# Zero products ahead of the first product, ScalarE's squares behind the weight copies, and the first group by two chunks, in a two-block transformer kernel on one core

## The chip, the cores and the metric

The kernel runs on 1 core of one Trainium2 chip. The metric is the device time of one execution in microseconds (us), the median of several runs. The core's engines are TensorE (PE in the profile; PEld is its weight load), VectorE (DVE), ScalarE (ACT), GpSimd (POOL) and SyncE (SP), which issues nearly all DMAs.

## The reference

A first block (windowed attention and a gated recurrence side by side, then an MLP) and a second block of two layers, on 256 tokens of width 1024 with 16 meta tokens ahead of them. What matters here is the first norm and the first projection:

```python
h = concat([meta_tokens, x])                 # 16 + 256 tokens of 1024
a = h * rsqrt(mean(h * h) + EPS) * norm_mix  # rms_norm
(q_na, k_na, v_na, q_hg, z_f, z_b, i_hg, g_hg, gate_na, gate_hg) = split(a @ w_in)
...                                          # both branches, w_o, MLP, second block
```

## The kernel before, in words

All matrix products run on TensorE from weights that come once from HBM. A weight is read in units of 512 rows by 512 columns (`units`, 1 MB of float32, tile `raw`), and each unit in two halves of two 128-row chunks. ScalarE copies a half into a rounded `whi` (L256), VectorE subtracts the copy from the raw half and leaves `wlo` (L257). The activations are split in the same way into a high part `xh` (ScalarE, L417) and a low part `xl` (VectorE, L418), transposed, so that a product of float32 accuracy is three products: high with high, high with low, low with high. The tokens are two tiles of 128 (t = 0, 1) and the 16 meta tokens; the width 1024 is two groups g of four chunks of 128 (tiles `xh_8`/`xl_9` are g = 0, `xh_10`/`xl_11` g = 1 in the kernel before).

The start runs like this. `norm_in(t)` squares a token tile on ScalarE (L442, a square and a read of its sum), VectorE adds the parts (L433), GpSimd takes the power, VectorE scales (L543, two halves of 512 columns) into `xn`. The scale vector is spread over the partitions by a product of a row of ones with `grow` (L514), which stays in two PSUM banks `g_ps` until the meta tokens are scaled. `split_in(t, g)` transposes four blocks on TensorE (L410) and splits the bank into `xh` and `xl`. `first_split(n)` cuts the nth half of the weights. `meta_in()` does the same for the meta tokens: its eight small transposes on TensorE are L571, and its splits write the last 16 columns of `xh` and `xl`.

The first product group is "gh" (`xstat_unit`, `xstat`: tokens are the stationary operand, 512 columns of weights move): 2 token tiles x 8 chunks x 3 = 48 products into two PSUM tiles. They are evicted by `ev_gh` (ScalarE L582, VectorE L583 and L584). The second group, "kn" (`wstat`, L361 to L363), takes all 272 tokens at once, so its first product needs the meta columns of `xh`, and the first with `xl` the meta columns of `xl`.

The order on each engine is set at build time by a scheduler, from the order in which the code is written, priorities (`urgent`) and `after(...)`, which keeps what is written under it behind given instructions. At run time every engine but TensorE's weight load goes through its own list in that order. The PSUM pool `mp` has four banks, two of them held by `g_ps` at the start. The order of SyncE's DMAs at the start is: first half of h[0], `grow`, second half of h[0], `ident`, first half of the first weight unit (L517), h[1] (L518), second half of that unit (L519), the two halves of the next unit, the meta tokens, `vrow`, the third unit.

Of the kernel before, what the change touches and what calls it, by code (L numbers as in the profile page):

```python
# [9 lines left out]
BF16 = mybir.dt.bfloat16  # L10
# [5 lines left out]
D = 1024  # L16
# [54 lines left out]
def kernel(  # L71
# [26 lines left out]
    def mt(i, shape, dt=F32, name="m"):  # L98
        return slot.tile(shape, dt, name=nm(name), tag=f"m{i}")
# [15 lines left out]
    def mps():  # L115
        return mp.tile([128, 512], F32, name=nm("mp"), tag="mp")
# [114 lines left out]
    for key, tags in BORROW.items():  # L231
        i = [u[0] for u in units].index(key)
# [110 lines left out]
        return [(q[k // 2][0][:, k % 2], q[k // 2][1][:, k % 2]) for k in range(4)]  # L343


    def xstat(ps, xs, ws, first, last):

        n = len(xs)
        for k in range(n):
            (xh, xl), (wh, wl) = xs[k], ws[k]  # L350
            T.matmul(ps, lhsT=xh, rhs=wh, start=first and k == 0, stop=False)  # L351
            T.matmul(ps, lhsT=xh, rhs=wl, start=False, stop=False)  # L352
            last_mm[:] = [T.matmul(ps, lhsT=xl, rhs=wh, start=False, stop=last and k == n - 1)]  # L353

    def wstat(ps, xs, ws, b, first, last):

# [23 lines left out]
    def tok(xT, k, t):  # L380
        hh, ll = xT[k // 4]
        return hh[:, k % 4, 128 * t:128 * t + 128], ll[:, k % 4, 128 * t:128 * t + 128]

    def xstat_unit(keys, xT, evict, budget=None, tfirst=False, ps=None):
        ps = ps or [acc(), acc()]
        if tfirst:
            ws = use(keys[0], budget) + use(keys[1], budget)
            for t in range(2):
                nl = len(later)
                xs = [tok(xT, k, t) for k in range(8)]  # L390
                xstat(ps[t], xs[:TF], ws[:TF], True, False)
                with flushed(nl):
                    xstat(ps[t], xs[TF:], ws[TF:], False, True)
                evict(t, ps[t])
        else:
            for i in range(2):
                ws = use(keys[i], budget)
                nl = len(later)
                for t in range(2):
                    with group():  # L400
                        xstat(ps[t], [tok(xT, 4 * i + k, t) for k in range(4)], ws, i == 0, i == 1)
                    if i == 1:
                        evict(t, ps[t])
                flush(nl)
# [9 lines left out]
    def split_bank(ps, hi, lo, scale=None):  # L414

        if scale is None:
            return (S.activation(out=hi, in_=ps, func=AF.Copy),  # L417
                    V.tensor_tensor(out=lo, in0=ps, in1=f(hi), op=ALU.subtract))  # L418
        else:
            S.activation(out=hi, in_=ps, func=AF.Copy, scale=scale)  # L420
            V.scalar_tensor_tensor(out=lo, in0=ps, scalar=scale, in1=f(hi), op0=ALU.mult, op1=ALU.subtract)
# [15 lines left out]
    def sq_mean(src, accum=None, of=None):  # L437

        n = src.shape[1]
        j = tmp.tile([128, 1024], BF16, name=nm("junk"), tag="junk", bufs=1)  # L440
        a = small([src.shape[0], 1], bufs=8) if accum is None else accum
        S.activation(out=j[0:src.shape[0], 0:n], in_=src, func=AF.Square, scale=float(of or n) ** -0.5, accum_out=a)  # L442
        return a
# [65 lines left out]
    nc.sync.dma_start(out=ident, in_=cst[:, C_ID:C_ID + 128])  # L509
    one_row = cp.tile([1, 128], F32, name="one_row")  # L510
    G.memset(one_row, 1.0)
    g_ps = [mps() for _ in range(2)]
    for k in range(2):
        T.matmul(g_ps[k], lhsT=one_row, rhs=grow[:, 512 * k:512 * k + 512], start=True, stop=True)  # L514
    w0 = rawp.tile([128, 2048], F32, name="raw0", tag="raw")
    w0v = w0.rearrange("p (k n) -> p k n", n=512)
    nc.sync.dma_start(out=w0v[:, 0:2], in_=units[0][1][:, 0:2])  # L517
# [12 lines left out]
          (mt(2, [128, 4, 272], F32R, "xh1"), mt(3, [128, 4, 272], F32R, "xl1"))]  # L530
    xn = [mt(5, [128, D], name="xn0"), mt(6, [128, D], name="xn1"), mt(7, [16, D], name="xnm")]

    def norm_in(t, src, parts):
        p = src.shape[0]
        q = small([p, 3])
        G.memset(q, EPS)
        for i in range(parts):
            n = D // parts
            sq_mean(src[:, n * i:n * i + n], q[:, i:i + 1], D)
        r = rpow(q[:, 0:parts + 1])  # L540
        for i in range(2):
            c = slice(512 * i, 512 * i + 512)
            V.scalar_tensor_tensor(out=xn[t][:, c], in0=src[:, c], scalar=r, in1=g_ps[i][0:p],  # L543
                                   op0=ALU.mult, op1=ALU.mult)

    def split_in(t, g):
        ps = transposes(xn[t][:, 512 * g:512 * g + 512]).rearrange("p (k t) -> p k t", k=4)
        c = slice(128 * t, 128 * t + 128)
        split_bank(ps, xT[g][0][:, :, c], xT[g][1][:, :, c])

    def first_split(n):
        cap[0] = n
# [2 lines left out]

    norm_in(0, h[0], 2)
    first_split(1)
    split_in(0, 0)
    first_split(2)
    norm_in(1, h[1], 1)  # L560
    split_in(1, 0)
    first_split(3)
    split_in(0, 1)
    first_split(4)
    split_in(1, 1)

    def meta_in():
        norm_in(2, hm, 1)
        ps = mps()
        for k in range(8):  # L570
            T.transpose(out=ps[:, 16 * k:16 * k + 16], in_=xn[2][:, 128 * k:128 * k + 128], identity=ident[0:16, 0:16])  # L571
        pv_ = ps[:, 0:128].rearrange("p (k t) -> p k t", k=8)
        for g in range(2):
            split_bank(pv_[:, 4 * g:4 * g + 4], xT[g][0][:, :, 256:272], xT[g][1][:, :, 256:272])
# [1138 lines left out]
```

## Time and profile before

| | |
|---|---|
| median of 3 runs | 845.84 us (845.59 to 846.05) |
| the profiled execution, its own time | 845.33 us |
| its span, first to last instruction | 843.4 us |
| TensorE busy | 828.1 us (98%) |
| VectorE, ScalarE, GpSimd busy | 581.4, 464.4, 59.2 us |
| mean granted TensorE clock in the records | 0.997 |
| first product of "gh" / of "kn" | 11.35 us / 26.91 us |

Times in the views count from the start of the span. "own time" is about 1.9 us longer than the span; what shifts the end of the span shifts it too.

### The profile page before, as it was taken

The page shows a single profiled execution, that of the slowest core. Times are in us where ns is not written, and L with a number is a line of the kernel's source. Part 1 is how long each engine was busy: PE and PEld are TensorE (multiplying, and loading weights), DVE is VectorE, ACT ScalarE, POOL GpSimd, SP SyncE. Part 2 cuts the span into 40 slices and gives each one's busy share as a digit, 9 for nine tenths or more (in the row PEclk, how much of TensorE's full clock was granted, in tenths as well). Part 3 has the DMA queues.
Part 4 walks back from the last instruction along what each step waited for, and adds up shares of the span by engine and source line. Part 5 has one row for each costly group of instructions (what it writes and reads, how often), then busy time and mean ns, then how long its engine had stood idle before and what let it go on. Part 6 is the DMA issues. An engine that isn't in the chain of part 4 may idle for free.

```text
span 843.4 us, 12871 instructions
## 1 busy us (share of the span) xinstructions
PE 828.1 (98%) x5037; PEld 734.7 (87%) x5037; DVE 581.4 (69%) x840; ACT 464.4 (55%) x757; POOL 59.2 (7%) x139
## 2 busy tenths in 40 slices
PE   6999999999999999999999999999999999999996
PEld 4999998888889999999879988888799999888885
DVE  6746667775859976657976868866655557559753
ACT  6456755574556655544775545545566455455442
POOL 2420020001000000000021000000000000020001
PEclk9999999999999999999999999999999999999998
DMA  8863443442549997867727556757155445559521
GB/s 304 259 195 106 151 151 101 160 158 82 199 131 361 373 334 274 299 224 274 258 94 252 198 192 224 257 200 249 67 205 172 154 149 172 165 198 318 175 82 50
DMA packets 88240, 168.02 MB, mean 199 GB/s; under 512 B 4802, under 2 KB 8898, under 8 KB 88180
## 3 DMA queue, kind: packets, MB, share of 16 engines
q1 hardware_dynamic: 87508, 166.66, 58.2%
q8 instruction: 39, 0.64, 0.3%
q10 hardware_dynamic: 288, 0.52, 0.2%
q14 instruction: 21, 0.17, 0.1%
q0 software_dynamic: 384, 0.03, 0.0%
HBM read 166.14 MB, written 1.05 MB: 198 GB/s over the span
## 4 chain that ended last, share of the span: by engine, by line
PE 93%; DVE 2%; DMA 1%; ACT 1%; issue 1%; POOL 0%; SPq 0%; POOLq 0%; DVEq 0%; ACTq 0%
PE acc L351 17%; PE acc L353 17%; PE acc L352 16%; PE acc L362 7%; PE acc L363 7%; PE acc L361 7%; PE mp L363 3%; PE mp L362 3%; PE mp L361 3%; PE mp L410 3%; PE mp L876 1%; DMA h<-in_x_dram 1%; ACT junk L442 1%; PE mp L353 1%; PE mp L351 1%
## 5 line engine op out<-in xcount | busy, mean ns | idle before, releaser
L257 DVE TENSOR_TENSOR wlo<-raw,whi 128x1024 fp32r<-128x1024 f32 x244 | 295.0, 1226 | 140.9 <-ACT whi L256 138.5
L256 ACT ACTIVATE whi<-raw 128x1024 fp32r<-128x1024 f32 x244 | 252.1, 1055 | 166.0 <-PE acc L353 101.3
L477 DVE SCALAR_TENSOR_TENSOR tb<-adw,csil,tb 128x512 f32<-128x512 f32 x96 | 71.1, 747 | 8.9 <-issue 4.9
L362 PE MATMUL acc<-xl,whi 128*128 128x272 f32 (+1 forms) x224 | 64.5, 288 | 0.0
L363 PE MATMUL acc<-xh,wlo 128*128 128x272 f32 (+1 forms) x224 | 64.5, 289 | 0.0
L361 PE MATMUL acc<-xh,whi 128*128 128x272 f32 (+1 forms) x224 | 64.3, 288 | 0.0
L361 PE MATMUL mp<-uh,whi 128*128 128x256 f32 x224 | 63.1, 285 | 0.0
L362 PE MATMUL mp<-ul,whi 128*128 128x256 f32 x224 | 63.0, 283 | 0.0
L363 PE MATMUL mp<-uh,wlo 128*128 128x256 f32 x224 | 62.1, 283 | 0.0
L363 PE MATMUL acc<-oh,wlo 128*128 128x256 f32 x192 | 55.0, 287 | 0.0
L362 PE MATMUL acc<-ol,whi 128*128 128x256 f32 x192 | 54.6, 284 | 0.0
L361 PE MATMUL acc<-oh,whi 128*128 128x256 f32 x192 | 54.4, 283 | 0.0
L351 PE MATMUL acc<-whi,hh 128*128 128x512 f32 x128 | 50.0, 392 | 0.0
L352 PE MATMUL acc<-wlo,hh 128*128 128x512 f32 x128 | 49.9, 390 | 0.0
L353 PE MATMUL acc<-whi,hl 128*128 128x512 f32 x128 | 49.7, 390 | 0.0
L351 PE MATMUL acc<-whi,yT 128*128 128x512 f32 (+1 forms) x128 | 48.5, 379 | 0.0
L352 PE MATMUL acc<-wlo,yT 128*128 128x512 f32 (+1 forms) x128 | 48.3, 377 | 0.0
L353 PE MATMUL acc<-whi,yT 128*128 128x512 f32 (+1 forms) x128 | 48.2, 377 | 0.0
L352 PE MATMUL acc<-wlo,oh 128*128 128x512 f32 x112 | 44.6, 398 | 0.0
L351 PE MATMUL acc<-whi,oh 128*128 128x512 f32 x112 | 44.3, 396 | 0.0
L352 PE MATMUL acc<-wlo,eh 128*128 128x512 f32 x112 | 44.0, 393 | 0.0
L353 PE MATMUL acc<-whi,ol 128*128 128x512 f32 x112 | 43.9, 392 | 0.0
(413 smaller groups left out, 2009.9 us busy)
## 6 DMA issues: line engine op xcount, KB each, us to landing
raw<-in_odd_in_w_dram SPq DMA_DIRECT2D x28, 1024.0 KB, 5.1
adw<-in_ada_w_dram SPq DMA_DIRECT2D x48, 512.0 KB, 6.1
raw<-in_w_in_dram SPq DMA_DIRECT2D x21, 1024.0 KB, 5.2
raw<-in_even_in_w_dram SPq DMA_DIRECT2D x20, 1024.0 KB, 5.1
raw<-in_w_up_dram SPq DMA_DIRECT2D x16, 1024.0 KB, 6.8
raw<-in_w_down_dram SPq DMA_DIRECT2D x16, 1024.0 KB, 7.3
raw<-in_even_out_w_dram SPq DMA_DIRECT2D x8, 1024.0 KB, 5.2
raw<-in_odd_out_w_dram SPq DMA_DIRECT2D x8, 1024.0 KB, 5.5
```

What stands on the lines that cost most here:

```text
L256: S.activation(out=hi.rearrange("p k n -> p (k n)"), in_=r, func=AF.Copy)
L257: V.tensor_tensor(out=lo.rearrange("p k n -> p (k n)"), in0=r, in1=f(hi.rearrange("p k n -> p (k n)")), op=ALU.subtract)
L351: T.matmul(ps, lhsT=xh, rhs=wh, start=first and k == 0, stop=False)
L352: T.matmul(ps, lhsT=xh, rhs=wl, start=False, stop=False)
L353: last_mm[:] = [T.matmul(ps, lhsT=xl, rhs=wh, start=False, stop=last and k == n - 1)]
L361: T.matmul(ps, lhsT=wh[:, c], rhs=xh, start=first and k == 0, stop=False)
L362: T.matmul(ps, lhsT=wh[:, c], rhs=xl, start=False, stop=False)
L363: T.matmul(ps, lhsT=wl[:, c], rhs=xh, start=False, stop=last and k == n - 1)
L410: last_t[:] = [T.transpose(out=ps[:, 128 * b:128 * b + 128], in_=src[:, 128 * b:128 * b + 128], identity=ident)]
L442: S.activation(out=j[0:src.shape[0], 0:n], in_=src, func=AF.Square, scale=float(of or n) ** -0.5, accum_out=a)
L477: V.scalar_tensor_tensor(out=a, in0=w[:, k], scalar=csil[:, kk:kk + 1], in1=a, op0=ALU.mult, op1=ALU.add)
L876: T.matmul(pss[i][:, 128 * hd:128 * hd + 128], lhsT=Kc[:, hd, 128 * i:128 * i + 128], rhs=bass.AP(tensor=q.tensor, offset=q.offset, ap=ap[ ...
```

## The change

Three things are done. (1) A zeroed bfloat16 tile `warm` is multiplied with itself on TensorE, 256 columns at a time, into PSUM banks that nobody reads: 9 products ahead of the two products with `grow`, 4 behind them, 5 behind the first four transposes. (2) ScalarE's squares of h[1] are put behind the first `xh`, those of the meta tokens behind the `xh` of token tile 0, g = 1. (3) For the first token tile and the first unit of "gh", `xstat` goes by two chunks: both high-high products, both high-low, both low-high, then the next two chunks. The number of products of the model is the same.

```diff
-    def xstat(ps, xs, ws, first, last):
+    def xstat(ps, xs, ws, first, last, by=1):
         n = len(xs)
-        for k in range(n):
-            (xh, xl), (wh, wl) = xs[k], ws[k]
-            T.matmul(ps, lhsT=xh, rhs=wh, start=first and k == 0, stop=False)
-            T.matmul(ps, lhsT=xh, rhs=wl, start=False, stop=False)
-            last_mm[:] = [T.matmul(ps, lhsT=xl, rhs=wh, start=False, stop=last and k == n - 1)]
+        for k0 in range(0, n, by):
+            ks = range(k0, k0 + by)
+            for m, (a, b) in enumerate(((0, 0), (0, 1), (1, 0))):
+                for k in ks:
+                    last_mm[:] = [T.matmul(ps, lhsT=xs[k][a], rhs=ws[k][b], start=first and k == 0 and m == 0,
+                                           stop=last and k == n - 1 and m == 2)]
...
-                        xstat(ps[t], [tok(xT, 4 * i + k, t) for k in range(4)], ws, i == 0, i == 1)
+                        xstat(ps[t], [tok(xT, 4 * i + k, t) for k in range(4)], ws, i == 0, i == 1,
+                              2 if keys[0] == ("gh", 0) and not i and not t else 1)
...
+    warm = mt(12, [128, 256], BF16, name="warm")
+    V.memset(warm, 0.0)
+    first = []
+    def warm_up(n):
+        ps = mps()
+        for _ in range(n):
+            with after(first):
+                first[:] = [T.matmul(ps[:, 0:256], lhsT=warm[:, 0:128], rhs=warm, start=True, stop=True)]
+    warm_up(9)
     g_ps = [mps() for _ in range(2)]
     for k in range(2):
-        T.matmul(g_ps[k], lhsT=one_row, rhs=grow[:, 512 * k:512 * k + 512], start=True, stop=True)
+        with after(first):
+            first[:] = [T.matmul(g_ps[k], lhsT=one_row, rhs=grow[:, 512 * k:512 * k + 512], start=True, stop=True)]
+    warm_up(4)
...
-    def norm_in(t, src, parts):
+    def norm_in(t, src, parts, behind=()):
...
-        for i in range(parts):
-            n = D // parts
-            sq_mean(src[:, n * i:n * i + n], q[:, i:i + 1], D)
+        with after(behind):
+            for i in range(parts):
+                n = D // parts
+                sq_mean(src[:, n * i:n * i + n], q[:, i:i + 1], D)
...
-    split_in(0, 0)
+    with after(first):
+        x00 = split_in(0, 0)
+    first[:] = last_t
+    warm_up(5)
     first_split(2)
-    norm_in(1, h[1], 1)
+    norm_in(1, h[1], 1, x00[:1])
     split_in(1, 0)
     first_split(3)
-    split_in(0, 1)
+    x01 = split_in(0, 1)
...
-        norm_in(2, hm, 1)
+        norm_in(2, hm, 1, x01[:1])
```

The built order on SyncE and GpSimd is the same in both kernels. On the other three it differs up to the start of "kn" and a little beyond, and not after that. Numbers behind a name are buffers: in the change `raw_121`, `raw_125`, `raw_131` are the first three weight units, `h_81` and `h_82` the two token tiles, `hm_128` the meta tokens, `mp_157`, `mp_184`, `mp_195`, `mp_206` the transposes of (t, g) = (0, 0), (1, 0), (0, 1), (1, 1), `acc_216` and `acc_217` the sums of "gh". Before, the same are `raw_104`, `raw_108`, `raw_114`, `h_81`, `h_82`, `hm_111`, `mp_140`, `mp_161`, `mp_172`, `mp_183`, `acc_193`, `acc_194`.

ScalarE at the start, from the second square of h[0], in the kernel before:

```order
L442 ACTIVATE junk_128,sm_124<-h_81 128x512
L256 ACTIVATE whi_136<-raw_104 128x1024
L442 ACTIVATE junk_153,sm_151<-h_82 128x1024
L417 ACTIVATE xh_8_117<-mp_140 128x4x128
L256 ACTIVATE whi_147<-raw_104 128x1024
L256 ACTIVATE whi_168<-raw_108 128x1024
L256 ACTIVATE whi_179<-raw_108 128x1024
L442 ACTIVATE junk_269,sm_267<-hm_111 16x1024
L417 ACTIVATE xh_8_117<-mp_161 128x4x128
```

The same place in the change:

```order
L444 ACTIVATE junk_145,sm_141<-h_81 128x512
L256 ACTIVATE whi_153<-raw_121 128x1024
L256 ACTIVATE whi_170<-raw_121 128x1024
L419 ACTIVATE xh_11_134<-mp_157 128x4x128
L444 ACTIVATE junk_176,sm_174<-h_82 128x1024
L256 ACTIVATE whi_191<-raw_125 128x1024
L256 ACTIVATE whi_202<-raw_125 128x1024
L256 ACTIVATE whi_218<-raw_131 128x1024
L419 ACTIVATE xh_11_134<-mp_184 128x4x128
```

The copy of the second half of the first unit now stands ahead of the first `xh`, and the squares of h[1] behind it; the copy of the third unit's first half stands ahead of the second `xh`.

VectorE from the first subtraction to the low part of (t, g) = (1, 0), before:

```order
L257 TENSOR_TENSOR wlo_137<-raw_104,whi_136 128x1024
L433 TENSOR_REDUCE sm_155<-sm_151 128x1
L418 TENSOR_TENSOR xl_9_118<-mp_140,xh_8_117 128x4x128
L543 SCALAR_TENSOR_TENSOR xn_13_122<-h_82,sm_156,mp_100 128x512
L543 SCALAR_TENSOR_TENSOR xn_13_122<-h_82,sm_156,mp_101 128x512
L257 TENSOR_TENSOR wlo_148<-raw_104,whi_147 128x1024
L257 TENSOR_TENSOR wlo_169<-raw_108,whi_168 128x1024
L257 TENSOR_TENSOR wlo_180<-raw_108,whi_179 128x1024
L433 TENSOR_REDUCE sm_271<-sm_267 16x1
L418 TENSOR_TENSOR xl_9_118<-mp_161,xh_8_117 128x4x128
```

The same stretch in the change:

```order
L257 TENSOR_TENSOR wlo_154<-raw_121,whi_153 128x1024
L560 SCALAR_TENSOR_TENSOR xn_15_138<-h_81,sm_148,mp_113 128x512
L257 TENSOR_TENSOR wlo_171<-raw_121,whi_170 128x1024
L420 TENSOR_TENSOR xl_12_135<-mp_157,xh_11_134 128x4x128
L435 TENSOR_REDUCE sm_178<-sm_174 128x1
L257 TENSOR_TENSOR wlo_192<-raw_125,whi_191 128x1024
L560 SCALAR_TENSOR_TENSOR xn_16_139<-h_82,sm_179,mp_112 128x512
L560 SCALAR_TENSOR_TENSOR xn_16_139<-h_82,sm_179,mp_113 128x512
L257 TENSOR_TENSOR wlo_203<-raw_125,whi_202 128x1024
L257 TENSOR_TENSOR wlo_219<-raw_131,whi_218 128x1024
L420 TENSOR_TENSOR xl_12_135<-mp_184,xh_11_134 128x4x128
```

The scaling of h[1] moved behind two more subtractions, and the low part of token tile 1 behind a subtraction of the third unit as well. On TensorE the transposes into `mp_206` wait for that low part, since they take the bank of `mp_184`.

ScalarE at the end of "gh" (`gg` is the eviction, the 128x4x16 rows are the meta columns), before:

```order
L256 ACTIVATE whi_229<-raw_227 128x1024
L256 ACTIVATE whi_233<-raw_227 128x1024
L417 ACTIVATE xh_8_117<-mp_277 128x4x16
L608 ACTIVATE csil<-vc 128x8
L582 ACTIVATE gg_190<-acc_193 128x512
L417 ACTIVATE xh_10_119<-mp_277 128x4x16
L604 ACTIVATE sm_297<-sm_294 128x8
L256 ACTIVATE whi_311<-raw_309 128x1024
L582 ACTIVATE gg_190<-acc_194 128x512
```

The same place in the change:

```order
L256 ACTIVATE whi_252<-raw_250 128x1024
L256 ACTIVATE whi_256<-raw_250 128x1024
L604 ACTIVATE gg_213<-acc_216 128x512
L256 ACTIVATE whi_334<-raw_332 128x1024
L604 ACTIVATE gg_213<-acc_217 128x512
L256 ACTIVATE whi_338<-raw_332 128x1024
L419 ACTIVATE xh_11_134<-mp_300 128x4x16
```

The meta columns moved behind both evictions of "gh" and two copies. On TensorE the eight small transposes that feed them stand ahead of the last 22 of the 48 products before, and behind all 48 in the change. On VectorE the meta columns of `xl` stand behind the subtraction that belongs to `whi_338`.

## Rows read from the trace of the kernel before

**Rows 1.** The page: span, then busy time of each engine.

```profile
span 843.4 us, 12871 instructions
PE 828.1 (98%) x5037; PEld 734.7 (87%) x5037; DVE 581.4 (69%) x840; ACT 464.4 (55%) x757; POOL 59.2 (7%) x139
```

**Rows 2.** Waits of TensorE, whole span: total us, times, longest.

```profile
PE acc L351 <- ACT xh L417: 3.1, 1, 3.1
PE mp L410 <- DVE xn L1228: 1.0, 2, 0.5
```

**Rows 3.** Timeline of ScalarE: start, us, instruction, idle time before it.

```profile
7.68 1.06 ACT L256 ACTIVATE whi<-raw 128x1024 fp32r<-128x1024 f32 x1 [2.23 <-DMA raw<-in_w_in_dram]
9.67 1.06 ACT L442 ACTIVATE junk<-h 128x1024 bf16<-128x1024 f32 x1 [0.94 <-DMA h<-in_x_dram]
10.63 0.19 ACT L442 ACTIVATION_READ_ACCUMULATOR junk<-h 128x1 f32 x1
10.72 0.58 ACT L417 ACTIVATE xh<-mp 128x512 fp32r<-128x512 f32 x1
11.20 1.04 ACT L256 ACTIVATE whi<-raw 128x1024 fp32r<-128x1024 f32 x1
...
21.69 1.05 ACT L256 ACTIVATE whi<-raw 128x1024 fp32r<-128x1024 f32 x1
22.63 0.20 ACT L417 ACTIVATE xh<-mp 128x64 fp32r<-128x64 f32 x1
...
27.11 0.60 ACT L582 ACTIVATE gg<-acc 128x512 f32<-128x512 f32 x1 [0.28 <-PE acc L353]
27.60 1.05 ACT L256 ACTIVATE whi<-raw 128x1024 fp32r<-128x1024 f32 x1
```

**Rows 4.** Timeline of TensorE, 11 to 28 us.

```profile
11.35 0.79 PE L351 MATMUL acc<-whi,xh 128*128 128x512 f32 x1 [3.06 <-ACT xh L417]
...
12.37 0.63 PE L353 MATMUL acc<-whi,xl 128*128 128x512 f32 x1
...
14.08 0.63 PE L351 MATMUL acc<-whi,xh 128*128 128x512 f32 x1
14.50 1.76 PE L410 MATMUL mp<-ident,xn 128*128 128x128 f32 x8
...
17.49 0.40 PE L352 MATMUL acc<-wlo,xh 128*128 128x512 f32 x1
...
18.39 0.39 PE L351 MATMUL acc<-whi,xh 128*128 128x512 f32 x1
...
20.71 0.40 PE L352 MATMUL acc<-wlo,xh 128*128 128x512 f32 x1
...
21.73 0.48 PE L351 MATMUL acc<-whi,xh 128*128 128x512 f32 x1
...
26.68 0.39 PE L353 MATMUL acc<-whi,xl 128*128 128x512 f32 x1
26.91 0.41 PE L361 MATMUL acc<-xh,whi 128*128 128x272 f32 x2
```

**Rows 5.** Timeline of VectorE, 8 to 17 us.

```profile
8.77 1.22 DVE L257 TENSOR_TENSOR wlo<-raw,whi 128x1024 fp32r<-128x1024 f32 x1 [0.97 <-ACT whi L256]
...
11.33 0.69 DVE L418 TENSOR_TENSOR xl<-mp,xh 128x512 fp32r<-128x512 f32 x1 [0.33 <-ACT xh L417]
11.94 1.40 DVE L543 SCALAR_TENSOR_TENSOR xn<-h,sm,mp 128x512 f32<-128x512 f32 x2
13.25 3.49 DVE L257 TENSOR_TENSOR wlo<-raw,whi 128x1024 fp32r<-128x1024 f32 x3
16.66 0.14 DVE L433 TENSOR_REDUCE sm<-sm 16x1 f32<-16x2 f32 x1
```

**Rows 6.** The DMA of L519, the first unit's second half: issue, then its landing.

```profile
3.39 0.44 SPq L519 DMA_DIRECT2D raw<-in_w_in_dram  x1
DMA to landing us min/median/max: 7.5/7.5/7.5
```

More of the change, by code (lines that the diff above doesn't have):

```diff
@@ L548, in split_in @@
         c = slice(128 * t, 128 * t + 128)
-        split_bank(ps, xT[g][0][:, :, c], xT[g][1][:, :, c])
+        return split_bank(ps, xT[g][0][:, :, c], xT[g][1][:, :, c])
     def first_split(n):
```

## The prediction

> **What bounds the kernel now.** I read the page first: TensorE is busy 828.1 of 843.4 us [rows 1]. The reader is to see that there are only some 15 us to win, and that a microsecond lost on TensorE is lost at the end. Then the waits of TensorE over the whole span: one of 3.1 us for the first `xh`, and after that none longer than 0.5 us [rows 2]. Behind the start the kernel therefore runs as fast as TensorE can, and the order there is the same in both kernels, so I take it that a shift of the start of "kn" goes through to the end one for one. The measure of the change is when TensorE gets to "kn": 26.91 us before [rows 4].
>
> The timeline of TensorE [rows 4] shows what the zero products are aimed at. The first products come every 0.43 us (12.37 to 14.08 is four of them), those from 18.39 to 20.71 every 0.232 us (ten). 512 columns in 0.43 us is the lower level of the clock, 1.2 GHz; 0.232 us is close to the upper, 2.4 GHz. Seven products and most of eight transposes (14.50, 1.76 us) ran at the lower level; at the upper they would have taken 7 x 0.232 + 8 x 0.11 = 2.5 us instead of about 4.9 (11.35 to 16.26). So at most 2.4 us is to be won by the clock.
>
> The timelines of ScalarE and VectorE [rows 3, 5] show what feeds TensorE. VectorE works without a pause from 11.33 us on (each row begins where the last ends). TensorE was slow just while its feed was thin, which is why no wait shows there.
>
> **The zero products.** 18 products of 256 columns. By the rows of 512 columns at either level one takes 0.12 to 0.21 us [rows 4]; their weight loads lie beside products there, so I price them at nothing. Nine take 1.0 to 1.9 us ahead of the products with `grow`; should they hold those up by all of it, the first transposes come as much later, and their `xh` has until 11.88 (below) instead of 10.72. The other nine stand in the 3.06 us in which TensorE waits for the first `xh` [rows 4], which grow longer. If the weight loads did not overlap it would be twice that, still inside the gap. The one memset on VectorE comes long before its first subtraction. Cost: 0.
>
> **ScalarE and the first product.** This is where the change costs. ScalarE takes its list in order, and now the copy of the first unit's second half stands ahead of the first `xh`. That half lands at 3.39 + 7.5 = 10.9 us [rows 6], and the order of the DMAs is the same. ScalarE, done with the first copy at 8.74, sits until 10.92. A following instruction starts 0.96 us after a copy or a long square, 0.09 after the read of a sum, 0.48 after an `xh` (starts 9.67, 10.63, 10.72, 11.20) [rows 3]. So: copy 10.92, `xh` 11.88 to 12.46, squares of h[1] 12.36, read 13.32, copy of the second unit's first half 13.41 to 14.47. The first product starts 0.05 us behind `xh`, at 12.5: 1.15 us later than before. The squares of h[1], which started at 9.67, start 2.7 us later.
>
> **VectorE and the second token tile.** Spacing on VectorE: a subtraction 1.137 us ((16.66 - 13.25)/3), a pair of scalings 1.31 (11.94 to 13.25), an `xl` 0.61 (11.33 to 11.94) and 0.69 long [rows 5]. The subtraction for the copy that ends at 14.47 starts at 14.50. Behind it in the new list: scalings of h[1] at 15.64, subtraction at 16.95, another, of the third unit, at 18.08, and only then `xl` of token tile 1, 19.22 to 19.91. The transposes of (1, 1) need the PSUM bank that this `xl` frees, so they start at 19.96. TensorE has by then done 12 products of token tile 0, 8 transposes and 4 more products, which take 12 x 0.232 + 8 x 0.11 + 4 x 0.232 = 4.6 us of the 7.45 us since 12.5. It stands idle about 2.9 us in several pieces: for `xl` of tile 0 (13.2 to 13.9 behind the second subtraction), for `xn` of tile 1 (first half done at about 16.4), for `xh` behind the third unit's copies.
>
> That makes the clock nearly worthless at this place: if the 12 products run at the lower level they take 12 x 0.195 = 2.3 us more, and nearly all of it falls into those waits. By my working 0.2 us comes through.
>
> From 19.96 TensorE runs through: four transposes 0.44 (17.49 to 18.39 less two products), 32 products x 0.232 = 7.43, the small transposes 0.79 (20.71 to 21.73 less one product) [rows 4]. That is 28.6 us, 1.7 us later than 26.91.
>
> **A new wait ahead of "kn".** Before, the meta tokens' small transposes stood 22 products ahead of "kn", and ScalarE split them at 22.63 [rows 3] under cover of those 22 x 0.232 = 5.1 us. Now they stand behind all 48 products, and their split stands on ScalarE behind the second eviction of "gh" and one more weight copy. The last product starts at 27.6 and its result is there 0.39 later (row of 26.68) [rows 4]: 28.0. Eviction 28.0; copy 0.49 behind it (27.11 to 27.60) at 28.5; small `xh` 0.96 behind that, 29.5 to 29.7 [rows 3]. TensorE, ready at 28.6, waits 1.1 us. It then has four products that need `xh` alone, 0.125 us each (26.91, two), up to 30.2. The next needs the meta columns of `xl`, which stand on VectorE behind the subtraction of that same copy: start 29.6 to 29.95 (VectorE comes from an eviction), 1.137 us, then about 0.2 us as for the small `xh`: 30.95 to 31.3. Second wait 0.75 to 1.1 us. TensorE goes on at about 31.15 with four products of "kn" done, as if it had begun at 30.65. Shift: 30.65 - 26.91 = 3.7 us.
>
> **The edit to two chunks** moves two products of `xl` and all use of the second half back, and adds none. What it could save, the wait of the third chunk, lies inside the stretch that VectorE sets. Cost 0. The squares of the meta tokens, now behind the `xh` of tile 0, g = 1, are followed by two more `xh` and subtractions long before the 27.8 at which their transposes come. Cost 0.
>
> **Sum.** 0 + 1.7 + 2.0 = +3.7, with 0 to 0.2 for a low clock: +3.8 us. The profiled execution took 845.33 us by its own time, so 849.1; the median shown is 0.5 above it, and I give the sum on the median: 849.6 us. A difference below 0.2% (1.7 us) counts here as about what a measurement of this kernel cannot tell from none.
>
> **The clock, trace against rule.** The trace shows a wait of 3.06 us ahead of 11.35 and the low level after it [rows 4]. The Trainium skill, "TensorE: Matmul & The Clock Gate", section "Part 1: The HAM clock gate", says that the low level is the default, that sustained activity lifts it, and that idleness brings it back. Here the gap behind the last zero products is longer than before (to 12.5), so by that rule they may buy nothing, and the new waits may even drop the clock later. By the rule the sum is +3.9 to +5.9, without it +3.7.
>
> **Rivals.**
> - *The clock falls again in the new waits.* TensorE idles 2.9 of 7.45 us from 12.5 on, and 2 of 2.5 us ahead of "kn". For it: the kernel before did run a stretch of about 4.6 us at the lower level (11.35 to about 16) [rows 4]. Against: no row shows the clock fall behind it. One more such stretch costs 4.6/2 = 2.3 us where TensorE would have been busy throughout, less where it waits: +5.1 to +5.9, on the median 850.9 to 851.7, about 851.3.
> - *The wait ahead of "kn" is not there* because the scheduler's list is met in another timing (evictions earlier, the copy done under the last products). Against it: the copy stands behind the eviction of the last product. Then only the shift of the start stays: +1.75, 847.6, at the very edge of what can be told.
> - *Not slower: the zero products hold the full clock and TensorE runs without waits from 12.5.* Then "kn" starts at 12.5 + 48 x 0.232 + 12 x 0.11 + 0.79 = 25.75, 1.15 us earlier: 844.7. It decides at the low part of token tile 1, which would have to be there at 17.1 instead of 19.9. Against it: VectorE's list from 8.77 [rows 5] up to that row holds five subtractions, three scalings, an `xl` and a small sum before it, 5 x 1.137 + 3 x 0.655 + 0.61 + 0.07 = 8.3 us, so 17.8 at the end even with no wait at all. To be told from no change it would need 0.5 us more.
>
> **Chances.** Forecast 0.55; clock falls again 0.22; no wait ahead of "kn" 0.12; not slower 0.11. The range takes in the first three, from the lower edge of the third (+1.6) to the upper of the second (+5.8): 847.4 to 851.6. Slower by over 0.2%: 0.55 + 0.22 + 0.07, a little over half of the 0.12, = 0.84. Within 0.2%: the other 0.05 and 0.07 of the last case, 0.12. Faster: 0.04, if that case also finds the 0.5 us.
>
> **What would show it.** In the changed profile: ScalarE idle from 8.7 to 10.9 ahead of its second copy; the first product at about 12.5; `xl` of token tile 1 ending near 19.9 and four transposes right behind it; then on TensorE two waits of about 1 us each at the start of "kn", for ScalarE's `xh` and for VectorE's `xl`; the fifth product of "kn" near 31.15. The clock: spacing of the first products 0.43 or 0.23 us, and no 0.43 behind 20 us. I am wrong if the first unit's second half lands much earlier than 10.9, if "kn" starts without those waits, or if a later part gives the shift back.

## The result, and the profile after

The changed kernel takes 850.1 us (median of 4 runs, 849.71 to 850.36), the kernel before in the same runs 845.72 (845.24 to 846.05). The ratio is 1.0056, 95% interval 1.0044 to 1.0068: 4.4 us slower, more than the 0.2% that this measurement can tell. The profiled execution of the change took 850.36 us. Its page begins:

```profile
span 848.5 us, 12911 instructions
PE 833.4 (98%) x5055; PEld 737.5 (87%) x5055; DVE 580.6 (68%) x841; ACT 464.6 (55%) x757; POOL 55.2 (7%) x139
```

Against [rows 1] the span is 5.1 us longer and TensorE holds 18 products more. The waits of TensorE in the first 40 us (total, times, longest) are now:

```profile
PE acc L353 <- ACT xh L419: 3.6, 3, 2.7
PE mp L523 <- DVE warm L516: 1.2, 1, 1.2
PE acc L362 <- ACT xh L419: 0.9, 1, 0.9
PE acc L363 <- DVE xl L420: 0.7, 1, 0.7
```

In [rows 2] stood one wait for the first `xh`. Now three stand there, and the two at L362 and L363 are the start of "kn". The timeline of ScalarE in the change (start, us, instruction, idle before) shows where the first come from:

```profile
8.41 1.06 ACT L256 ACTIVATE whi<-raw 128x1024 fp32r<-128x1024 f32 x1 [3.06 <-DMA raw<-in_w_in_dram]
10.99 1.06 ACT L256 ACTIVATE whi<-raw 128x1024 fp32r<-128x1024 f32 x1 [1.52 <-DMA raw<-in_w_in_dram]
11.95 0.58 ACT L419 ACTIVATE xh<-mp 128x512 fp32r<-128x512 f32 x1
12.43 1.05 ACT L444 ACTIVATE junk<-h 128x1024 bf16<-128x1024 f32 x1
...
18.59 0.60 ACT L419 ACTIVATE xh<-mp 128x512 fp32r<-128x512 f32 x1 [1.76 <-PE mp L412]
19.08 1.05 ACT L256 ACTIVATE whi<-raw 128x1024 fp32r<-128x1024 f32 x1
20.03 0.59 ACT L419 ACTIVATE xh<-mp 128x512 fp32r<-128x512 f32 x1
...
29.29 0.60 ACT L604 ACTIVATE gg<-acc 128x512 f32<-128x512 f32 x1 [0.28 <-PE acc L353]
29.79 1.05 ACT L256 ACTIVATE whi<-raw 128x1024 fp32r<-128x1024 f32 x1
30.74 0.21 ACT L419 ACTIVATE xh<-mp 128x64 fp32r<-128x64 f32 x1
```

The second copy waits for its half until 10.99, and the first `xh` stands behind it (11.95, in [rows 3] 10.72). At the end one eviction and one copy stand ahead of the meta columns' `xh` at 30.74. TensorE in the same execution:

```profile
12.59 1.22 PE L353 MATMUL acc<-whi,xh 128*128 128x512 f32 x2 [2.69 <-ACT xh L419]
...
17.02 1.05 PE L353 MATMUL acc<-whi,xl 128*128 128x512 f32 x2
17.87 1.12 PE L412 MATMUL mp<-ident,xn 128*128 128x128 f32 x8
19.24 0.50 PE L353 MATMUL acc<-whi,xh 128*128 128x512 f32 x1 [0.25 <-ACT xh L419]
...
21.24 0.60 PE L412 MATMUL mp<-ident,xn 128*128 128x128 f32 x4
...
31.00 0.76 PE L362 MATMUL acc<-xh,whi 128*128 128x272 f32 x4 [0.88 <-ACT xh L419]
32.47 0.39 PE L363 MATMUL acc<-xl,whi 128*128 128x272 f32 x1 [0.70 <-DVE xl L420]
```

All 12 first products came 0.43 us apart (12.59 to 17.87), the lower of the two levels, 1.2 GHz. The transposes of (1, 1) started at 21.24, and VectorE was not what they waited for: its `xl` of token tile 1 ended at 19.96.

```profile
17.01 2.36 DVE L257 TENSOR_TENSOR wlo<-raw,whi 128x1024 fp32r<-128x1024 f32 x2
19.28 0.68 DVE L420 TENSOR_TENSOR xl<-mp,xh 128x512 fp32r<-128x512 f32 x1
...
31.06 1.22 DVE L257 TENSOR_TENSOR wlo<-raw,whi 128x1024 fp32r<-128x1024 f32 x1
32.20 0.22 DVE L420 TENSOR_TENSOR xl<-mp,xh 128x64 fp32r<-128x64 f32 x1
```

"kn" goes on from its fifth product at 32.47, as if it had begun at 32.47 - 4 x 0.125 = 31.97, 5.06 us later than in [rows 4]. That is the whole difference of the spans: nothing is won or lost behind it.

### The profile page after: what moved, and what is told of

Same layout as the page of the kernel before. It is cut to its first block, busy times and chain, and to the rows that moved or that the text cites. A ratio compares the mean times of both kernels' runs of the same rounds, so it can differ in the third digit from the quotient of the medians.

```text
span 848.5 us, 12911 instructions
## 1 busy us (share of the span) xinstructions
PE 833.4 (98%) x5055; PEld 737.5 (87%) x5055; DVE 580.6 (68%) x841; ACT 464.6 (55%) x757; POOL 55.2 (7%) x139
## 4 chain that ended last, share of the span: by engine, by line
PE 92%; DVE 3%; ACT 2%; DMA 1%; issue 1%; POOL 0%; SPq 0%; POOLq 0%; DVEq 0%; ACTq 0%
PE acc L353 49%; PE acc L363 7%; PE acc L364 7%; PE acc L362 7%; PE mp L363 3%; PE mp L362 3%; PE mp L364 3%; PE mp L412 3%; PE mp L353 2%; PE mp L898 1%; DMA raw<-in_w_in_dram 1%; DVE wlo L257 1%; DMA raw<-in_even_in_w_dram 1%; PE mp L734 1%; ACT junk L444 1%
## 5 line engine op out<-in xcount | busy, mean ns | idle before, releaser
L353 PE MATMUL acc<-whi,yT 128*128 128x512 f32 (+1 forms) x256 | 76.6, 378 | 0.0
L363 PE MATMUL acc<-xl,whi 128*128 128x272 f32 (+1 forms) x224 | 64.7, 289 | 0.7 <-DVE xl L420 0.7
L362 PE MATMUL acc<-xh,whi 128*128 128x272 f32 (+1 forms) x224 | 64.2, 289 | 0.9 <-ACT xh L419 0.9
L362 PE MATMUL mp<-uh,whi 128*128 128x256 f32 x224 | 63.1, 285 | 0.0
L363 PE MATMUL mp<-ul,whi 128*128 128x256 f32 x224 | 63.0, 283 | 0.0
L353 PEld LDWEIGHTS acc<-whi,yT 128*128 128x128 f32 x256 | 47.3, 188 | 8.8
L363 PE MATMUL acc<-ol,whi 128*128 128x256 f32 x192 | 54.6, 284 | 0.0
L362 PE MATMUL acc<-oh,whi 128*128 128x256 f32 x192 | 54.4, 283 | 0.0
```

The costliest lines, as they stand in the source:

```text
L353: last_mm[:] = [T.matmul(ps, lhsT=xs[k][a], rhs=ws[k][b], start=first and k == 0 and m == 0, stop=last and k == n - 1 and m == 2)]
L362: T.matmul(ps, lhsT=wh[:, c], rhs=xh, start=first and k == 0, stop=False)
L363: T.matmul(ps, lhsT=wh[:, c], rhs=xl, start=False, stop=False)
```

## The experiments

Twelve kernels in three groups of four: no_zero to no_meta_behind as they stand in the table, squares_only to copy_behind_xh, clock_held to the end. Each was measured beside the kernel before on the same chip, whose medians were 845.39, 845.14 and 845.55 us, so kernels of different groups are best compared by their ratios. Times in us; "first", "(1, 1)" and "kn" are where TensorE starts the first product of "gh", the transposes of (1, 1) and the first product of "kn" in the profile ("in pieces": two products of "kn" start at 23.13, among those of "gh", the others from 28.10 on).

| kernel | first | (1, 1) | "kn" | span | median | ratio to before, interval |
|---|---|---|---|---|---|---|
| before | 11.35 | 17.72 | 26.91 | 843.4 | 845.72 | |
| the change | 12.59 | 21.24 | 31.00 | 848.5 | 850.1 | 1.0056, 1.0044 to 1.0068 |
| no_zero | 10.04 | 17.55 | 26.64 | 843.1 | 844.34 | 0.9991, 0.9982 to 0.9999 |
| zero_only | 12.26 | 20.05 | 29.36 | 846.3 | 848.65 | 1.0036, 1.0023 to 1.0050 |
| order_kept | 12.60 | 21.17 | 30.25 | 846.9 | 848.79 | 1.0037, 1.0025 to 1.0050 |
| no_meta_behind | 12.84 | 20.69 | 29.41 | 846.1 | 848.37 | 1.0034, 1.0021 to 1.0047 |
| squares_only | 9.73 | 17.24 | 26.31 | 842.7 | 844.61 | 0.9993, 0.9985 to 1.0002 |
| chunks_only | 11.14 | 18.95 | in pieces | 844.1 | 846.53 | 1.0013, 1.0004 to 1.0022 |
| zero_gap | 10.05 | 17.57 | 26.64 | 843.0 | 844.88 | 0.9996, 0.9987 to 1.0005 |
| copy_behind_xh | 10.07 | 19.69 | 30.76 | 848.7 | 851.47 | 1.0076, 1.0062 to 1.0090 |
| clock_held | 12.45 | 19.88 | 29.71 | 849.5 | 851.53 | 1.0077, 1.0065 to 1.0090 |
| no_chunks | 12.78 | 21.64 | 31.41 | 849.1 | 851.02 | 1.0070, 1.0058 to 1.0083 |
| tile1_early | 9.46 | 16.23 | 25.70 | 842.0 | 844.00 | 0.9985, 0.9976 to 0.9994 |
| tile1_early_gap | 9.68 | 15.55 | 25.08 | 841.5 | 843.78 | 0.9983, 0.9975 to 0.9992 |

### Which edit costs: the zero products, by the lists

**no_zero**, the change without edit 1:

```diff
-    warm_up(9)
...
-    warm_up(4)
...
-    warm_up(5)
```

> The change without its 18 zero products. ScalarE's list then has the first `xh` right behind the first weight copy, the squares of h[1] behind it, and only then the copy that waits for the landing at 10.9; the meta columns' split stands on ScalarE between the two evictions of "gh". List theory (the zero products cost by the place that the scheduler gives the second copy because of them, not by their own time): first `xh` at about 9.7, first product at about 10.3, the fifth product of "kn" without a wait of 0.7 us ahead of it, "kn" at about 26 us, so about 1 us faster than before: 844.7 us, ratio to before 0.9988. Squares theory (the squares of h[1] and of the meta tokens, moved back, are what makes token tile 1 and the meta columns late): still 3 us or more above before, 849 us. Clock theory (the late rise of TensorE's clock at 18.0 us is the main loss, and the zero products bring it): the rise comes near 16 us again and 2 us come back, 848 us.

The list theory holds: 844.34 us. Edits 2 and 3 alone do not cost anything; they win about 1 us (0.8 by the ratio). TensorE and VectorE in this kernel:

```profile
10.04 1.22 PE L353 MATMUL acc<-whi,xh 128*128 128x512 f32 x2 [1.77 <-ACT xh L419]
...
17.55 0.66 PE L412 MATMUL mp<-ident,xn 128*128 128x128 f32 x4 [0.23 <-DVE xl L420]
```

```profile
13.41 3.49 DVE L257 TENSOR_TENSOR wlo<-raw,whi 128x1024 fp32r<-128x1024 f32 x3
16.81 1.28 DVE L420 TENSOR_TENSOR xl<-mp,xh 128x512 fp32r<-128x512 f32 x2
```

Here VectorE sets the pace: three subtractions, then the `xl` for which the transposes of (1, 1) wait.

**zero_only**, the change without edits 2 and 3:

```diff
-                              2 if keys[0] == ("gh", 0) and not i and not t else 1)
+                              1)
...
-    norm_in(1, h[1], 1, x00[:1])
+    norm_in(1, h[1], 1)
...
-        norm_in(2, hm, 1, x01[:1])
+        norm_in(2, hm, 1)
```

> The zero products alone; squares and the order of the first group's products as before. On ScalarE the squares of h[1] stand where they stood, but the second weight copy still stands ahead of the first `xh`; the meta columns' split stands between the two evictions of "gh". List theory: first product at 12.4 to 12.6 as in the change (the copy waits for 10.9), token tile 1 not much later than before, no wait ahead of the fifth product of "kn"; "kn" 1 to 2 us later than before, 847 us. Squares theory: nothing but a small shift, within 0.5 us of before, 846 us. Theory that the zero products help by the clock: first products 0.23 us apart, and 1 to 2 us faster than before, 844 us.

Edit 1 alone costs 3 us, more than any theory said. The first product comes at 12.26, as the list theory has it. But TensorE's products stay 0.43 us apart until 17.95 (before: until about 16), which the list theory did not count; together they move "kn" by 2.45 us (29.36 - 26.91). The span is 2.9 us longer; most of the rest stands in two waits for `xn` far behind "kn" (1.4 us, in [rows 2] 1.0).

**order_kept**, no zero products, but the first `xh` behind the second copy (`hl_a[1]`) by hand:

```diff
-    warm_up(9)
...
-    warm_up(4)
...
-    with after(first):
+    first_split(2)
+    with after([hl_a[1]]):
         x00 = split_in(0, 0)
-    first[:] = last_t
-    warm_up(5)
-    first_split(2)
```

> No zero products, but the first `xh` is put behind the second weight copy by hand, and the squares of h[1] behind it, as they stand in the change; the first eight instructions of ScalarE's list are those of the change. Further down the list the copies of the third unit stand ahead of the second `xh`, and the meta columns' split between the evictions of "gh". List theory: the loss of the change at the start stays without a single zero product: first product at 12.5 to 12.6, token tile 1 late, "kn" at 29 to 30.5 us, 848 to 849 us. Theory that the zero products cost by themselves (their time, or their effect on the clock): the loss goes, 846 us or less.

This settles what kind of cost it is. Without a single zero product the loss at the start is there again: 848.79 against 844.34 us for the same edits with the `xh` ahead. In the lists that follow from it, `xl` of token tile 1 stands behind three subtractions that start only at 17.02:

```profile
17.02 3.49 DVE L257 TENSOR_TENSOR wlo<-raw,whi 128x1024 fp32r<-128x1024 f32 x3
20.43 1.28 DVE L420 TENSOR_TENSOR xl<-mp,xh 128x512 fp32r<-128x512 f32 x2
```

In the change only two subtractions stand there, and its `xl` ended at 19.96. That the transposes of (1, 1) start at 21.17 here and at 21.24 in the change is in part chance: here they wait 1.12 us for VectorE, there for a chain on ScalarE. The run shows that the order of the lists is enough for such a loss, not that the same row sets it.

**copy_behind_xh**, the whole change with all 18 zero products, the copies put back behind the first `xh`:

```diff
-    first_split(2)
+    with after(x00[:1]):
+        first_split(2)
```

> The whole change with its 18 zero products, but the weight copies from the second on are put behind the first `xh`. On ScalarE the first `xh` stands ahead of the copy that waits for the landing at 10.9; the squares of h[1] still stand behind that copy, the third unit's copy ahead of the second `xh`, and the meta columns' split behind both evictions of "gh". Theory A (the first product's delay by the one copy is the loss at the start): first product at about 10.3, the wait of 1.6 us ahead of "kn" stays, 847 us. Theory B (what counts is when token tile 1 comes, and its squares and `xh` stand where they stood): the first product comes at about 10.3, but the transposes of (1, 1) not before 19.5 to 21, "kn" near 30.5, and the time stays near that of the change, 849 us.

Theory B holds in its rows: the first product comes 2.5 us earlier than in the change, and the transposes of (1, 1) come at 19.69, "kn" at 30.76. What counts is token tile 1. Its squares still stand behind the copy, its `xh` behind the third unit's copy (17.00), and TensorE waits for it. In that wait the clock falls; the answer by stretches (length, TensorE's busy time and instructions, granted clock, DMA share, GB/s) shows it:

```profile
14.00:16.00 2.00, 1.63 (x12) 1.00 1.05 372
16.00:18.00 2.00, 0.55 (x3) 0.95 1.05 389
18.00:20.00 2.00, 1.89 (x6) 0.50 1.03 353
20.00:22.00 2.00, 2.00 (x9) 0.70 1.03 388
```

The median, 851.47, is 2.5 us above what theory B said and 1.4 us above the change, and these rows do not explain that: at "kn" this kernel is 0.24 us ahead of the change. Behind "kn" it waits 0.6 us longer for `xn` and `oh` (1.6 against 1.0 us in all), and its profiled execution took 2.7 us more than its span, in the change 1.9; why stays open.

### The wait ahead of "kn"

**no_meta_behind**, the meta tokens' squares free again:

```diff
-        norm_in(2, hm, 1, x01[:1])
+        norm_in(2, hm, 1)
```

> The change, but with the squares of the meta tokens where the scheduler puts them freely (ahead of the third unit's copy, as before). The first 11 instructions of ScalarE's list are those of the change; the meta columns' `xh` stands ahead of the evictions of "gh", and the small transposes ahead of the last products. Theory of the prediction (two separate losses, the late start and the wait ahead of "kn"): first product at 12.59 as in the change, no wait at the first and at the fifth product of "kn", and the 0.9 + 0.7 us of waits with the 0.8 us small transposes moved under cover give some 2 us back: 848 us, "kn" at about 29. Rival (the meta columns' wait is only the place at which a loss shows that token tile 1 causes): the time is that of the change, 850 us, with the wait moved elsewhere.

As the prediction's theory has it: 848.37 us, and no wait at L362 or L363. "kn" starts at 29.41, 2.56 us ahead of the 31.97 above; 0.55 of that was won before the transposes of (1, 1) (20.69 against 21.24), so by the profile the place of the meta columns is worth 2.0 us. The term was 2.0. By the medians the two kernels differ by 1.7 us in all, so 2.0 is its upper end. The 0.55 us stand where the clock differed:

```profile
12.84 0.73 PE L353 MATMUL acc<-whi,xh 128*128 128x512 f32 x2 [2.85 <-ACT xh L419]
13.41 0.98 PE L353 MATMUL acc<-wlo,xh 128*128 128x512 f32 x2
14.22 1.22 PE L353 MATMUL acc<-whi,xl 128*128 128x512 f32 x2
15.24 1.05 PE L353 MATMUL acc<-whi,xh 128*128 128x512 f32 x2
```

The first two products take 0.57 us (12.84 to 13.41), the upper level; from 14.22 us on they are 0.43 us or more apart. In the change, with the same zero products ahead, the first two took 1.02 us.

### The other two edits

**squares_only** is no_zero with the products in the old order, **chunks_only** the kernel before with edit 3 alone, **no_chunks** the change with this edit taken back:

```diff
-                              2 if keys[0] == ("gh", 0) and not i and not t else 1)
+                              1)
```

> Of the three edits only the second, ScalarE's squares behind the splits. ScalarE's and VectorE's lists up to the second eviction of "gh" are those of the change without zero products (844.34 us); only TensorE's first products stand in the old order. Theory that the gain without zero products comes from the squares' place: the same time, 844.3 us, first `xh` right behind the first copy, token tile 1's `xl` behind three subtractions. Theory that the two chunks bring it: no gain, 845.4 us.

> Of the three edits only the third, the first token tile's products by two chunks. The prediction priced it at 0. But the built lists differ from before: on VectorE the `xl` of token tile 1 now stands behind a subtraction of the third unit and the two scalings of the meta tokens, 1.14 + 1.3 us by the rows of before. List theory: those 2.4 us reach TensorE's transposes of (1, 1), which need the bank that this `xl` frees, so "kn" starts some 2 us later and the time is about 847.5 us. Theory of the prediction (the order of six products costs nothing): within 0.5 us of before, 845.4 us.

> The change without its third edit: the first token tile's products in the old order. Copies of the third unit, splits and evictions stand on ScalarE as in the change but for the meta tokens' squares and the 16-column splits by a place or two; the meta columns' split still stands behind both evictions of "gh" and two copies. By the prediction (third edit costs 0): 850 us, first product 12.6, two waits ahead of "kn". Theory that the third edit costs here what it cost alone (1.4 us): 848.7 us.

squares_only equals no_zero within the intervals, so the gain without zero products comes from the squares' place and not from the chunks; the gain is small, and the interval of squares_only alone still takes in 1. chunks_only is 1.4 us slower than before: the order of six products is free, but the lists built around it are not. `xl` of token tile 1 comes behind a fourth subtraction and the meta scalings, at 19.49. The transposes of (1, 1) do not wait for it, as the list theory had it: they start at 18.95, before it, behind the first of the meta scalings (0.22 us put down to `xnm`). The next product takes an `xl` and comes at 20.21; the theory's time was 847.5 us. Within the change this does not recur: without edit 3 it is no faster (1.0070, overlapping 1.0056).

### What the clock is worth

**zero_gap**, no_zero with 8 zero products between the first transposes and the first product, all else in the same order:

```diff
+            with after(behind), tc.high_priority(offset=-LOW):
+                T.matmul(ps[:, 0:256], lhsT=warm[:, 0:128], rhs=warm, start=True, stop=True)
...
+    warm_up(8, first)
```

> The change without its 18 zero products, but with 8 of them put right behind the first transposes, at a low priority, so that every other instruction on TensorE, ScalarE and VectorE stands as in the kernel without zero products (844.34 us). TensorE is then busy from the first transposes at about 7.2 us to the first product at about 10. Theory that zero products lift the clock as other products do and that VectorE sets the pace of the start: the 0.43 us spacing of the first products ends near 13 us or earlier instead of 16.2, and yet the transposes of (1, 1) come near 17.5 as before, because `xl` of token tile 1 ends there; time 844 us, no more than 0.5 us less. Theory that the clock is worth its 2 us: 842.5 us. Theory that zero products do not lift it: 0.43 us until about 16, 844.3 us.

```profile
7.93 1.91 PE L523 MATMUL mp<-warm 128*128 128x256 bf16 x8
10.05 1.17 PE L353 MATMUL acc<-whi,xh 128*128 128x512 f32 x2 [0.21 <-ACT xh L419]
11.06 0.62 PE L353 MATMUL acc<-wlo,xh 128*128 128x512 f32 x2
...
17.57 0.66 PE L412 MATMUL mp<-ident,xn 128*128 128x128 f32 x4 [0.30 <-DVE xl L420]
```

The first theory holds in its rows: from the third product on two products take some 0.46 us (11.06 to 11.52), the upper level, 2.4 GHz, four us earlier than without zero products (no_zero: about 15.2). And the transposes of (1, 1) come at 17.57 as they did at 17.55, and the time is the same within the intervals (0.9996 against 0.9991). In this order the clock buys only waits.

**clock_held**, the change with the pause ahead of the first product filled, the lists as in the change:

```diff
-            S.activation(out=hi.rearrange("p k n -> p (k n)"), in_=r, func=AF.Copy)
+            with after(x10[:1] if i == 5 else ()):
+                S.activation(out=hi.rearrange("p k n -> p (k n)"), in_=r, func=AF.Copy)
...
-    warm_up(5)
+    warm_up(18)
...
-    split_in(1, 0)
+    x10[:] = split_in(1, 0)
```

> The change with 13 more zero products behind the first four transposes (18 in place of 5), and the copy of the third unit's second half written behind the second `xh`, where it stands in the change anyway, so that every other instruction on TensorE, ScalarE and VectorE stands as in the change. TensorE's pause ahead of the first product at 12.59 falls from 2.7 us to less than 1. Theory that the late rise of the clock (18.0 us) cost the change about 1.3 us: the 12 first products come every 0.23 us, the transposes of (1, 1) near 20.0 instead of 21.24, and the time is 848.8 us; the two waits ahead of "kn" stay. Theory that the wait lists set the pace and the clock is worth nothing here either: 850 us, the transposes of (1, 1) near 21. Theory that the higher level does not last through the waits between 15.5 and 20 us: 0.43 us spacing once more near 18 to 21 us, and 849.5 us or more.

```profile
12.45 0.73 PE L356 MATMUL acc<-whi,xh 128*128 128x512 f32 x2 [0.81 <-ACT xh L422]
...
19.88 0.66 PE L415 MATMUL mp<-ident,xn 128*128 128x128 f32 x4
...
29.71 0.76 PE L365 MATMUL acc<-xh,whi 128*128 128x272 f32 x4 [0.89 <-ACT xh L422]
31.17 0.59 PE L366 MATMUL acc<-xl,whi 128*128 128x272 f32 x1 [0.70 <-DVE xl L423]
31.57 0.43 PE L367 MATMUL acc<-xh,wlo 128*128 128x272 f32 x1
```

Up to "kn" the first theory holds: 1.3 us are won (19.88 against 21.24, 29.71 against 31.00), 0.14 of it with the first product. But the time is not lower, it is 1.4 us higher. The granted clock in the stretches behind it says where the gain went:

```profile
30.00:32.00 2.00, 1.30 (x7) 0.72 1.16 264
32.00:34.00 2.00, 2.00 (x10) 0.50 0.96 172
34.00:36.00 2.00, 2.00 (x17) 0.93 0.93 333
```

In the two waits ahead of "kn" the clock fell, as the prediction's first rival has it, and the first dozen of its products ran 0.22 us apart in place of 0.125, which takes back 12 x 0.1 = 1.2 us. That alone would leave the time of the change. The 1.0 us by which the span is longer stands in one wait for `xn`, 1.32 us at 430.14 (in the change 0.31 us at 429.08). `xn` is late because two weight copies ahead of it are, first in the change, then in clock_held:

```profile
420.62 2.01 ACT L256 ACTIVATE wb<-raw 128x1024 fp32r<-128x1024 f32 x2 [1.56 <-DMA raw<-in_even_in_w_dram]
421.68 2.01 ACT L259 ACTIVATE wb<-raw 128x1024 fp32r<-128x1024 f32 x2 [2.09 <-DMA raw<-in_even_in_w_dram]
```

What makes their weights land 1.1 us later, no run here explains.

### A version faster than both

**tile1_early** is no_zero with the fourth weight copy behind the `xh` of (1, 0), **tile1_early_gap** the same with the 8 zero products of zero_gap:

```diff
-            S.activation(out=hi.rearrange("p k n -> p (k n)"), in_=r, func=AF.Copy)
+            with after(x10[:1] if i == 3 else ()):
+                S.activation(out=hi.rearrange("p k n -> p (k n)"), in_=r, func=AF.Copy)
...
-    split_in(1, 0)
+    x10[:] = split_in(1, 0)
```

> The change without zero products (844.34 us), and the fourth weight copy written behind the `xh` of (1, 0). On VectorE the `xl` of token tile 1 then stands behind two subtractions instead of three, 1.14 us earlier. Theory that VectorE's list alone sets the start in the kernel without zero products: the transposes of (1, 1) come near 16.5 to 17 instead of 17.55 and the time falls by up to 1 us, 843.5 us. Theory that now TensorE at the low level is the limit (its first 12 products and 8 transposes run until 16.2): no gain, 844.3 us.

> As the kernel with token tile 1 earlier, and in addition the 8 zero products behind the first transposes, which brought the higher level at about 11 us. Theory that the clock and token tile 1's low part bound the start together, each hiding the other: this one gains though either alone gains nothing; "kn" near 25.1 to 25.9 us and 843.3 us, some 1 us below the kernel without zero products. Theory that the clock is worth nothing at this place in any order: 844.3 us, like the three kernels before it.

Both are faster than the kernel before, by 1.5 and 1.8 us (844.00 and 843.78 against 845.55). That the two edits help only together isn't shown: tile1_early alone has most of the gain, and its interval overlaps those of no_zero and of tile1_early_gap. The profiles point to the mechanism all the same. In tile1_early `xl` of token tile 1 ends at 16.02 and TensorE, slow until about 14.8, gets to the transposes of (1, 1) at 16.23: TensorE is the limit. In tile1_early_gap, with the upper level from about 13.2 us on, `xl` ends at 15.49 and the transposes come at 15.55, with TensorE done with the products ahead at about the same time: neither waits for the other.

## Why the prediction was right, and which term was mis-sized

1. **Zero products cost 0 by their own time.** Right: order_kept has their loss without them, zero_gap has 8 of them without the loss. (Four of the nine that the prediction put into the wait for the first `xh` stood ahead of the first transposes, which came at 7.77 us instead of 7.18; `xh` stood behind the copy until 11.95 all the same.) That they cost by the list that they make the scheduler build stood under ScalarE in the prediction, and no_zero and order_kept show it: putting the first `xh` behind the second copy, with all that the scheduler then moves, is worth 4.4 us (848.79 against 844.34) with the same edits. It is not the one `xh` by itself: copy_behind_xh has it ahead of the copy again and is no faster.
2. **The first product at 12.5, `xl` of token tile 1 from 19.22 to 19.91.** 12.59, and 19.28 to 19.96. The list theory of both engines holds to 0.1 us. The first wait is put down to ScalarE, as forecast.
3. **"By my working 0.2 us comes through" of the low clock.** This is the mis-sized term: 1.3 us came through. The 2.3 us of slow products did not all fall into waits for VectorE. The transposes of (1, 0) stand behind those products and ended late (17.87 and on), and behind them runs a chain on ScalarE that the prediction had only as "for `xh` behind the third unit's copies": `xh` 18.59, copy 19.08, `xh` 20.03, TensorE's product 20.67, and then the transposes at 21.24, 1.3 us behind VectorE's 19.96. clock_held shows it: with the clock up ahead of the first product, the transposes come at 19.88, "kn" at 29.71 and its fifth product at 31.17, where the prediction had 19.96, 29.7 and 31.15.
4. **A wait of 2.0 us ahead of "kn".** Waits of 0.88 and 0.70 us at the two places, for the two tiles named; no_meta_behind gets up to 2.0 us back.
5. **Edit 3 costs 0, the meta squares cost 0.** In the change, yes for the first; alone it costs 1.4 us by its lists. The squares themselves cost nothing, but their place is what put the meta columns behind the evictions.
6. **Sum.** 1.7 + 1.3 + 2.1 = 5.1 us by the profiles, against 3.8 forecast; the 2.1 is what is left, and some 0.2 of it is not a wait (TensorE took 8.9 us from the transposes of (1, 1) until it was ready for "kn", 8.6 by the forecast). By the medians it is 4.4: the change's profiled execution lay 0.26 us above its median, that of before 0.39 below. So it is partly luck that 850.1 us came out only 0.5 above the forecast of 849.6: against the profile that it was worked out from, the sum was 1.3 us short. That a shift of "kn" goes through to the end one for one held in the change, but not in clock_held and copy_behind_xh, where waits far behind "kn" grew.

Of the rivals, the fall of the clock in the new waits did not occur in the change (0.125 us spacing from 32.70 on), but it did in clock_held ahead of "kn", where the slow products took 1.2 us (the prediction had 1.3 to 2.1 for it), and in copy_behind_xh in the wait for token tile 1, where its price is not told apart. In the change the 18 zero products bought nothing ahead of the first product: the level was the lower one before the pause of 2.69 us and after it.

The Trainium skill, "TensorE: Matmul & The Clock Gate", section "Part 1: The HAM clock gate", has it that activity lifts the level and idleness brings it back. The traces agree on the first in zero_gap, where two products take 0.46 us from 11.06 on, and on the second in no_meta_behind, where the first two products behind a pause of 2.85 us came 0.29 us apart and those from 14.22 on 0.43 us and more. The change does not bear out the first: its level stayed low through 8.7 us of almost unbroken work ahead of the pause.

## What to carry to other kernels

Instructions that cost nothing where they run can cost through the order that a scheduler builds around them, so compare the built lists of every engine with and without each edit. Before pinning an instruction, find the row that sets the pace: here the first `xh`, put back in its place by itself, won nothing. A faster clock is worth only what the next feeder lets through: find out which list sets the next row before pricing it. And a wait that one edit makes can lose the clock that another edit has bought, so the two are to be priced together.

## What the runs showed of the hardware that was not expected

- Products of zeros can lift the clock, but when is not fixed: with the same eight, the spacing fell to 0.23 us at about 11.0 us in zero_gap and at about 13.2 us in tile1_early_gap (without them between about 14 us in squares_only and 15.2 in no_zero). With the same 18 the first product found the upper level in no_meta_behind (12.84) and the lower one in the change (12.59).
- Short pauses can cost the level, and need not. Behind the same two waits ahead of "kn" (0.9 and 0.7 us) it fell in clock_held and stayed in the change. In the change TensorE was busy from 1.20 to 9.89 us with hardly a pause, and the four transposes at 7.77 us still came 0.21 us apart, the lower level.
- The column of the granted clock can say 1.00 where the spacing of the products says otherwise. From 14 to 16 us products stand 0.43 us or more apart in both the change (the first answer below, 1.00) and no_meta_behind (the second, 0.50), so the start has to be read by the spacing:

```profile
14.00:16.00 2.00, 2.00 (x6) 1.00 1.05 386
```

```profile
14.00:16.00 2.00, 2.00 (x5) 0.50 1.03 371
```

- The first weight half landed at another time in nearly every profile. ScalarE's first copy, which waits for it, started between 7.51 (chunks_only) and 8.73 us (no_meta_behind), though the DMAs ahead of it are the same in all kernels, so single timelines are uncertain by some tenths of a us, and small gains are read from the medians.
